# Attention matmuls in 64-row tiles throughout: 64x64 for the scores, 64x32 for values and sums

## The chip, the cores and the metric

The kernel runs as one program on all eight cores of one Trainium2 chip. The cores divide the batch and do not talk to each other. The metric is the device time of the slowest core in microseconds (us). Most executions agree within 0.3%, but a program on eight cores has a second, slower state. In it the cores of one die, sometimes of both, get a lower TensorE clock, and the time is some per cent longer, whatever the kernel. "Mean of the cores" below is the mean of the eight core spans of one profiled fast run. It is steadier than the slowest core, which hops from core to core between runs.

## The reference, cut to what matters

One layer of a streaming encoder: RMS norm, one input projection, two mixers side by side (attention in a sliding window, and a gated MLP that mixes positions in chunks of 128), a gated merge, and a SwiGLU feed-forward. The change touches the attention of the long prompts. There are 16 query heads of 64 and 4 key/value heads; a chunk of 64 queries sees its own chunk and the two before it, and each head has a "sink" in the denominator:

```python
def sink_attention(q, k, v, sinks, mask):
    s = jnp.einsum('...qhgd,...khd->...hgqk', q, k).astype(jnp.float32) * (HEAD_DIM ** -0.5)
    ...
    p = jnp.exp(s - m)
    denom = jnp.sum(p, axis=-1, keepdims=True) + jnp.exp(sk - m)
    p = (p / denom).astype(v.dtype)
    return jnp.einsum('...hgqk,...khd->...qhgd', p, v)
```

A core has two prompts of 4096 rows. It works on them in 16 tiles (t0 to t15) of 512 rows, and each tile in four blocks of 128 rows: 64 blocks. A block has two query chunks (c = 0, 1). Each sees 192 keys: one pair of key chunks lies wholly inside the windows and is done as 128 rows, the third key chunk as 64 rows.

## The kernel before: the parts that matter

The scores are computed transposed (keys on partitions). `PT` holds the exponentials of the 128-key part, `PT3` those of the third key chunk. Values and denominators (a product with a matrix of ones) follow as matmuls. `ps` is PSUM, with eight banks of 128 x 512 FP32.

```python
def S2(b):                                   # scores and exponentials of one block
    for tp in range(2):
        for c in range(2):
            for h in range(2):
                kc0 = c0 + 128 * c
                mm(v4(ps[:, 2 * tp + h, 256 * c:256 * c + 256]),      # tile 64 x 128
                   kT[64 * h:64 * h + 64, tp, kc0:kc0 + 128], qv(tp, h, c), ...)
        act(PT[:, tp, :, cs], ps[:, 2 * tp:2 * tp + 2, cs], AF.Exp, ...)
    ...                                      # third chunk: tiles of 64 x 64, banks 4 and 5
    act(PT3[pr], ps[pr, 4:6, :], AF.Exp, B(4, 5), ["PT3"], scale=0.125)

def PV(n):                                   # 128 x 64 tiles: values, then sums, of the two full chunks
    for use_v in (True, False):
        for c in range(2):
            for h in range(2):
                o = ps[hs, pb + c, 0:256] if use_v else ps[hs, pb + c, 256:512]
                lhs = Vt[:, b + c, vc] if use_v else ones[:, 0:64]
                mm(o, lhs, PT[:, tp, h, 256 * c:256 * c + 256], ...)
    small.append(lambda: PVs(b, tp, first))  # 64 x 64 tiles with PT3: run after both PV calls

def divide(b, tp):                           # twice per block
    act(od, ps[:, pb:pb + 2, :], AF.Copy, ...)
    tt(POOL, d4, d4, esb, ALU.add, ...)
    recip(od[:, :, 256:512], od[:, :, 256:512], ok_, ok_)   # VectorE, 128 x 512
    mults[tp] = ...
```

This is the loop over the four blocks of a tile (G = 0 to 3, which I call blocks 1 to 4), and the order of the gelu units ahead of it:

```python
steps = "v0 v0 u0 v1 v1 u1 u2 v2 v2 u3 b0 u4 s0 b1 u5 s1 | b2 v3 s2 v3 u6 u7".split()   # u, v: gelu
...
for G in range(4):
    S2(G)                                    # scores, exponentials
    ...
    for j, (bl, hf) in enumerate(sp[G]):
        if G:
            seed(hf, 4 + j)                  # ScalarE writes a bias into a PSUM bank
    g_unit(4 * G)                            # 8 dense matmuls of 512 columns, then a tanh on ScalarE
    ...
    g_unit(4 * G + 1)
    PV2(G)                                   # values and sums
    ...
    g_unit(4 * G + 2)
    if N and N["turned"]:
        if G in (1, 2):
            turned_square(N, G)              # ScalarE squares rows of the next tile
    ...
    g_unit(4 * G + 3)
    if N and N["turned"] and G == 0:
        turned_square(N, 0)
```

The softmax here doesn't subtract the row's maximum and nothing guards it: scores larger than these inputs give would overflow.

## Time and profile before

| before | value | view |
|---|---|---|
| time, 3 runs | 4013.2 fast; 4354.0 and 4628.99 slow | times |
| spans of the cores, profiled run (fast) | 4008.7 to 4015.0, mean 4011.2 us | table of cores |
| granted TensorE clock | 0.997 to 0.999 | table of cores |
| TensorE / VectorE / ScalarE / GpSimd busy | 99% / 44% / 35% / 20% | page |
| attention matmuls of the prompts, busy | 229 us, 5.7% | list of groups |

From the page of the profiled run: the busy time of the engines, the chain of work that ended last, and one group (line, engine, operation, out<-in, shapes, count | busy us, mean ns | idle before and its releaser).

```profile
span 4015.0 us, 60008 instructions; the slowest of 8 cores (4008.7 to 4015.0 us)
...
PE 3962.1 (99%) x22234; PEld 1893.3 (47%) x22630; DVE 1752.7 (44%) x1725; ACT 1390.4 (35%) x2144; POOL 806.8 (20%) x1028
...
PE 97%; issue 1%; DMA 1%; DVE 0%; ACT 0%; POOL 0%; DVEq 0%; SPq 0%; POOLq 0%; ACTq 0%
...
L334 DVE RECIPROCAL tmp<-tmp 128x512 f32<-128x512 f32 x129 | 421.9, 3311 | 127.4 <-POOL tmp L319 127.3
...
```

TensorE is busy 99% of the span and makes up 97% of the chain. Only time that TensorE itself saves counts directly; the VectorE reciprocals, although they add up to 422 us, are not on the chain.

One block on TensorE, from the timeline (start us, length us, engine, line, operation, out<-in, tile, shapes, count):

```profile
...
2086.73 0.95 PE L300 MATMUL ps<-qT,kT 64*128 64x256 bf16 x16
2087.61 3.63 PE L300 MATMUL ps<-hT,ring 128*128 128x512 bf16 x16
2091.17 0.41 PE L300 MATMUL ps<-PT,Vt 128*64 128x256 bf16 x4
2091.41 0.38 PE L300 MATMUL ps<-PT,ones 128*64 128x256 bf16 x4
2091.63 0.39 PE L300 MATMUL ps<-PT,Vt 128*64 128x256 bf16 x4
2091.85 0.39 PE L300 MATMUL ps<-PT,ones 128*64 128x256 bf16 x4
2092.16 0.30 PE L300 MATMUL ps<-PT,Vt 64*64 64x256 bf16 x4
...
2092.51 0.28 PE L300 MATMUL ps<-PT,ones 64*64 64x256 bf16 x4
2092.73 0.62 PE L300 MATMUL ps<-WmT,mgT 128*128 128x128 bf16 x8
```

The length of a group contains the flow of its last matmul, so I read starts. From the first score (2086.73) to the next dense matmul (2087.61) is 0.88 us; from the first value (2091.17) to the next work (2092.73) is 1.56 us. A "round" is a set of matmuls that use different parts of the array at the same time; a round of 256 columns takes 0.109 us. Before, a block has 4 + 2 rounds of scores and 8 + 4 rounds of values and sums.

This is block 1 of tile t9, ScalarE and then TensorE:

```profile
...
2323.04 0.60 ACT L309 ACTIVATE big<-ps 128x512 bf16<-128x512 f32 x1 [1.13 <-PE ps L300]
2323.66 1.28 ACT L309 ACT_TABLE_LOAD   x1
2324.95 2.85 ACT L309 ACTIVATE PT<-ps 128x1024 bf16<-128x1024 f32 x3
...
```

### The profile page before, as it was taken

How to read it: one execution, taken by the hardware profiler on the slowest of the kernel's cores; microseconds unless marked ns; L12 is line 12 of the kernel's file. 1: busy time of each engine (PE TensorE's matmuls, PEld its weight loads, DVE VectorE, ACT ScalarE, POOL GpSimd, SP SyncE). 2: the span in 40 equal slices, each digit the busy share in tenths (PEclk: the TensorE clock that was granted, in tenths of full speed). 3: DMA queues.
4: the chain of work that ended last, by engine and by line, in shares of the span. 5: the costliest groups of instructions: out<-in, count | busy, mean ns of one | idle time of the engine just before them, and what ended most of it. 6: DMA issues, size and time to landing. Idle time of an engine off the chain costs nothing.

```text
span 4015.0 us, 60008 instructions; the slowest of 8 cores (4008.7 to 4015.0 us)
## 1 busy us (share of the span) xinstructions
PE 3962.1 (99%) x22234; PEld 1893.3 (47%) x22630; DVE 1752.7 (44%) x1725; ACT 1390.4 (35%) x2144; POOL 806.8 (20%) x1028
## 2 busy tenths in 40 slices
PE   8999999999999999999999999999999999999998
PEld 4544445444444444444444444444444444444444
DVE  4616426163361633616345262442615426163352
ACT  5515325153241423314243142522515224152331
POOL 3204123040220302202031120311203012030220
PEclk9999999999999999999999999999999999999999
DMA  9999998885664645537455464654646445464442
GB/s 174 186 186 210 193 200 217 216 236 160 195 202 154 223 153 181 194 138 232 147 192 184 144 211 163 203 168 161 209 148 208 168 171 198 150 219 151 176 145 81
DMA packets 128326, 727.58 MB, mean 181 GB/s; under 512 B 20142, under 2 KB 22666, under 8 KB 58538
## 3 DMA queue, kind: packets, MB, share of 16 engines
q1 hardware_dynamic: 105088, 603.72, 44.3%
q0 software_dynamic: 15856, 95.57, 14.9%
q10 hardware_dynamic: 7098, 24.42, 1.5%
q8 instruction: 188, 3.08, 0.3%
q14 instruction: 96, 0.79, 0.1%
HBM read 749.06 MB, written 70.08 MB: 204 GB/s over the span
## 4 chain that ended last, share of the span: by engine, by line
PE 97%; issue 1%; DMA 1%; DVE 0%; ACT 0%; POOL 0%; DVEq 0%; SPq 0%; POOLq 0%; ACTq 0%
PE ps L300 96%; PE ps L304 1%; DMA gx<-xp 0%; DMA s_rs<-stt 0%; DVE tmp L330 0%; ACT PT L309 0%; DMA aT<-vecs 0%; DVE hT L330 0%; DMA hst<-s_rs 0%; POOL stt L319 0%; DVE big L330 0%; ACT hst L309 0%; ACT big L309 0%; SPq L136 0%; DVE hst L330 0%
## 5 line engine op out<-in xcount | busy, mean ns | idle before, releaser
L300 PE MATMUL ps<-aT,ring 128*128 128x512 bf16 (+1 forms) x6551 | 1446.0, 378 | 9.6 <-ACT aT L309 1.4
L309 ACT ACTIVATE tmp<-ps 128x512 f32<-128x512 f32 (+2 forms) x614 | 463.1, 765 | 1612.9 <-PE ps L300 1611.7
L300 PEld LDWEIGHTS ps<-aT,ring 128*128 128x128 bf16 x6704 | 655.2, 98 | 774.1 <-issue 1.6
L300 PE MATMUL ps<-hT,ring 128*128 128x512 bf16 x4206 | 965.7, 379 | 12.2 <-issue 3.2
L319 DVE TENSOR_TENSOR big<-ps,tmp 128x512 bf16<-128x512 f32 x352 | 243.2, 691 | 972.4 <-PE ps L300 920.3
L300 PEld LDWEIGHTS ps<-hT,ring 128*128 128x128 bf16 x4352 | 414.1, 98 | 485.8 <-issue 19.9
L300 PE MATMUL ps<-ring,big 128*128 128x512 bf16 x2756 | 605.8, 379 | 3.2
L326 POOL TENSOR_SCALAR stt<-stt 128x1 f32<-128x1 f32 (+2 forms) x289 | 139.0, 481 | 2186.0 <-ACT tmp L309 1777.9
L334 DVE RECIPROCAL tmp<-tmp 128x512 f32<-128x512 f32 x129 | 421.9, 3311 | 127.4 <-POOL tmp L319 127.3
L330 DVE SCALAR_TENSOR_TENSOR tmp<-ps,stt,gS 128x1024 f32<-128x1024 f32 x123 | 157.9, 1283 | 700.0 <-POOL stt L319 679.9
L300 PEld LDWEIGHTS ps<-ring,big 128*128 128x128 bf16 x2816 | 275.2, 98 | 332.6 <-issue 1.3
L300 PE MATMUL ps<-ring,hT 128*128 128x512 bf16 (+1 forms) x1518 | 293.2, 344 | 1.1 <-issue 0.2
L309 ACT ACTIVATE big<-ps 128x512 bf16<-128x512 f32 (+1 forms) x389 | 226.0, 596 | 190.3 <-PE ps L300 186.8
L300 PE MATMUL ps<-big,ring 128*128 128x512 bf16 x1021 | 235.4, 379 | 1.3 <-DVE tmp L330 1.1
L300 PE MATMUL ps<-ring,mgT 128*128 128x512 bf16 x1008 | 225.9, 379 | 2.0 <-DVE mgT L319 1.2
L309 ACT ACTIVATE qT<-ps 128x512 bf16<-128x512 f32 (+1 forms) x132 | 80.1, 606 | 412.0 <-PE ps L300 411.7
L300 PEld LDWEIGHTS ps<-ring,hT 128*128 128x128 bf16 x1536 | 148.1, 98 | 124.2 <-issue 1.3
L319 POOL TENSOR_TENSOR stt<-stt,negh 128x1 f32<-128x1 f32 (+1 forms) x292 | 184.4, 632 | 52.6 <-DVE stt L326 8.7
L319 POOL TENSOR_TENSOR aT<-tmp 128x512 bf16<-128x512 f32 x112 | 142.1, 1269 | 257.6 <-DVE tmp L334 253.3
L309 ACT ACTIVATE PT<-ps 128x1024 bf16<-128x1024 f32 (+1 forms) x192 | 180.7, 1018 | 0.3
L330 DVE SCALAR_TENSOR_TENSOR tmp<-big,ps 128x1024 f32<-128x1024 bf16 x128 | 155.5, 1215 | 54.8 <-PE ps L300 54.8
L319 POOL TENSOR_TENSOR xt<-xt,tmp 128x1024 f32<-128x1024 f32 x60 | 141.6, 2360 | 92.2 <-DVE tmp L330 92.2
(164 smaller groups left out, 2289.6 us busy)
## 6 DMA issues: line engine op xcount, KB each, us to landing
ring<-s_wfi SPq DMA_DIRECT2D x145, 1024.0 KB, 5.5
ring<-s_win SPq DMA_DIRECT2D x136, 1024.0 KB, 6.1
ring<-wb POOLq DMA_DIRECT2D x84, 1024.0 KB, 19.0
ring<-s_wfo SPq DMA_DIRECT2D x58, 1024.0 KB, 4.8
xt<-xp SPq DMA_DIRECT2D x63, 512.0 KB, 11.3
ring<-s_wap SPq DMA_DIRECT2D x30, 1024.0 KB, 7.3
ring<-s_wgp SPq DMA_DIRECT2D x29, 1024.0 KB, 7.4
ring<-s_wout SPq DMA_DIRECT2D x29, 1024.0 KB, 8.8
```

The source lines that it names most:

```text
L300: m.op(PE, lambda e: e.matmul(out, lhsT=lhsT, rhs=rhs, start=start, stop=stop, skip_group_check=True), reads=reads, writes=[("ps", bank)])
L304: m.op(PE, lambda e: e.transpose(out=out, in_=in_, identity=idn), reads=reads + ["ident"], writes=[("ps", TB)])
L309: m.op(ACT, lambda e: e.activation(out=out, in_=in_, func=func, scale=scale, **kw), reads=reads, writes=writes)
L319: m.op(eng, lambda e: e.tensor_tensor(out=out, in0=in0, in1=in1, op=op), reads=reads, writes=writes)
L326: m.op(eng, lambda e: e.tensor_scalar(out=out, in0=in0, scalar1=s1, scalar2=s2, op0=op0, op1=op1), reads=reads, writes=writes)
L330: m.op(DVE, lambda e: e.scalar_tensor_tensor(out=out, in0=in0, scalar=scalar, in1=in1, op0=op0, op1=op1), reads=reads, writes=writes)
L334: m.op(DVE, lambda e: e.reciprocal(out=out, in_=in_), reads=reads, writes=writes)
```

## The change

The intent: use only tiles of 64 rows, so that the array is cut the same way throughout a stage and more tiles run at once. Scores become 64x64 (four tiles at once, still six rounds). Values and sums become 64x32: eight tiles at once, nine rounds instead of twelve. Sums now lie in banks of their own (2 and 3), which saves one reciprocal, one eviction and two GpSimd adds per block and costs two VectorE adds. The two row halves never write one bank at the same time: each writes a bank of its own, and halfway they exchange banks; the exchange is guarded by a wait of TensorE on its own semaphore.

```diff
-                        for h in range(2):
-                            kc0 = c0 + 128 * c
-                            mm(v4(ps[:, 2 * tp + h, 256 * c:256 * c + 256]),
-                               kT[64 * h:64 * h + 64, tp, kc0:kc0 + 128], qv(tp, h, c), True, True, KK + QK,
-                               2 * tp + h)
+                        for j in range(2):
+                            for h in range(2):
+                                kc0 = c0 + 128 * c + 64 * j
+                                mm(v4(ps[64 * j:64 * j + 64, 2 * tp + h, 256 * c:256 * c + 256]),
+                                   kT[64 * h:64 * h + 64, tp, kc0:kc0 + 64], qv(tp, h, c), True, True, KK + QK,
+                                   2 * tp + h)
...
+                def tiles(which, out, lhs, lk):        # one round: 2 row halves x 4 heads
+                    for r in range(2):
+                        rs = slice(64 * r, 64 * r + 64)
+                        c = (0, 1, r)[which]           # which 0, 1: PT; 2: PT3
+                        ...
+                        for k in range(4):
+                            ...
+                            mm(ps[32 * k:32 * k + 32, bank, 256 * c:256 * c + 256], lhs(rs, sl, k, r), p, ...)
...
+                sums(0)
+                values(0, 0)
+                values(0, 1)
+                values(0, 2)                           # fourth round: needs PT3
+                swap_at = len(m.ops[PE]) - 1
+                sums(1)
+                sums(2)
+                if ordered:
+                    m.self_wait(PE, swap_at)
+                values(1, 0)                           # row halves write the other's bank
+                values(1, 1)
+                values(1, 2)
...
+                act(od, ps[:, 0:2, :], AF.Copy, B(0, 1), ok_)
+                tt(DVE, v4(t), v4(ps[:, 2, :]), esb, ALU.add, B(2) + ["es2"], tk)
+                tt(DVE, t[:, cs], ps[:, 3, cs], t[:, cs], ALU.add, B(3) + tk, tk)
+                recip(t, t, tk, tk)
```

Cut: the same for the short sample rows, the new order of the sinks and of the projection's rows that follows from the 32-column tiles, and the small method that records the self-wait.

## The prediction

> All times are for the fast state: before 4013.2 us, 4015.0 us in the profile, granted clock 0.998.
>
> **What bounds the kernel.** TensorE: busy 99% of the span, and 97% of the chain of waits. VectorE is busy 44%, ScalarE 35%, GpSimd 20%. Only time that TensorE itself saves or loses counts.
>
> **Attention on TensorE now.** The attention matmuls (qT·kT, PT·Vt, PT·ones, two shapes each) are busy 229 us, 5.7% of the span (list of groups). The timeline from 2086 to 2093 us shows one block of 128 rows: scores start at 2086.73, the next dense matmul at 2087.61 (0.88 us); values and sums start at 2091.17, the next work at 2092.72 (1.55 us). A block repeats every 10.0 us; there are 64.
> Matmuls on different tiles run together: one round of 256 columns, whether two 128x64, two 64x128 or four 64x64 tiles, takes 0.109 us (start to start). Before: 4+2 rounds of scores, 8+4 of values and sums. The Trainium skill ("TensorEngine Tiling (Array Packing)", Key Properties) says that a change of tiling mode drains the array. The trace agrees: over a change, start to start is about 0.09 us longer than a round, and the next round 0.02 longer. There are six changes per block.
>
> **What the change does on TensorE.** Scores are 64x64 throughout: six rounds, one mode change less. Values and sums become 72 matmuls of 64x32, eight tiles at once: nine rounds instead of twelve, one change less. Four 32-column tiles did run together in the sample rows (0.22 us per four at 512 columns); I expect eight to. Instruction supply should hold: the trace shows a matmul and its weight load dispatched in about 9 ns, so 8 pairs need 75 ns of a round's 109.
> Saved per block: 3 x 0.109 + 2 x 0.115 = 0.56 us.
> Lost: the skill's Restrictions (Gotcha 1) say that different row tiles may not use one bank at once, hence the self-wait. Its matmul lies two rounds before it. A matmul ends 0.27 us after its start and a semaphore needs about 0.1 us to be seen and passed, against 0.33 us of cover: an estimated 0.10 us lost per block. The third exponential ends 0.1 us after values start today and will be needed 0.35 us after; it should just fit.
> Net 0.46 us x 64 = 29 us.
>
> **Elsewhere, off the path.** Per block one reciprocal of 128x512 less (3.31 us VectorE), two adds from PSUM more (0.69 us each): VectorE about -120 us. ScalarE loses one 1.0 us eviction per block, GpSimd two 1.0 us adds (-130 us). Score banks 2 and 3 are now freed by VectorE, about 0.5 us before the next scores want them. Weights are only reordered; the sample path is negligible.
>
> **Predicted:** 3984 us (-0.7%), 3968 to 4006. Faster by over 2%: 0.02; within 2%: 0.96; slower: 0.02.
>
> **What would show it.** Blocks repeat every 9.5 to 9.6 us. Scores to next dense about 0.78 us, values and sums to the next work about 1.2 us. Eight 64x32 matmuls start within 0.03 us; rounds 0.11 us apart, one gap of 0.2 us at the self-wait. Reciprocals x65 instead of x129; VectorE busy about 1630 us, GpSimd about 680.
>
> **What would make it wrong.** Eight tiles not running together, or 144 instructions in 1 us starving the queue: values and sums stay at 1.5 us and nothing is gained. A late third exponential or late VectorE adds, as PE idle with those as releaser. A self-wait costing 0.3 us or more. A lower granted clock from denser array use.

## More of the kernel before

```profile
...
2327.32 0.41 PE L300 MATMUL ps<-PT,Vt 128*64 128x256 bf16 x4
...
2328.32 0.30 PE L300 MATMUL ps<-PT,Vt 64*64 64x256 bf16 x4
...
```

The last gelu of the tile is followed by a load of ScalarE's function table (1.28 us), and only then do the three exponentials run, until 2327.80. Values start at 2327.32, so the third exponential is 0.48 us late for a start of values. It does no harm here, because the old order uses it only in the last four rounds, at 2328.32, 1.00 us after values start.

## The result, and the profile after

The changed kernel ran in 4003.42, 4003.16 and 4003.45 us, and once in the slow state (4696.96; die 1 had a clock of 0.837). In the same rounds the kernel before took 4013.2 and 4012.5 us fast (4354.0 and 4628.99 slow). The ratio of the fast runs is 0.9976, with a 95% interval of 0.9953 to 0.9998. Here and below a ratio is the mean time of one kernel's fast runs over that of the other's fast runs of the same rounds, so it is not quite the ratio of the medians quoted. The forecast was "within 2%", which is right, and 4003.4 lies in the stated range. But the gain is 0.24%, a third of the 0.7% that was forecast: about 10 us on the slowest core and 12.7 us in the mean of the cores of the two profiled runs (4011.2 to 3998.5), instead of 29. Over all undisturbed fast runs the kernel before has means of 4008.8 to 4011.4 and the changed kernel, in its three fast runs here, 3998.5 to 3998.9, so the gain is 10 to 13 us.

The page after, the same parts, with the queue that brings instructions (packets, MB, share):

```profile
span 4001.9 us, 66201 instructions; the slowest of 8 cores (3995.3 to 4001.9 us)
...
PE 3966.1 (99%) x25670; PEld 1879.1 (47%) x25670; DVE 1630.8 (41%) x1790; ACT 1333.1 (33%) x2080; POOL 678.6 (17%) x900
...
q8 instruction: 211, 3.46, 0.3%
...
PE 97%; ACT 1%; issue 1%; DMA 1%; DVE 0%; POOL 0%; DVEq 0%; POOLq 0%; ACTq 0%
...
L342 DVE RECIPROCAL tmp<-tmp 128x512 f32<-128x512 f32 (+1 forms) x65 | 215.5, 3316 | 6.7
...
```

The reciprocals are x65, VectorE is busy 1630.8 us and GpSimd 678.6 us, as predicted. TensorE is still 99% busy. The queue q8 moved 188 packets before and 211 now: each is 16,384 bytes, and the 23 more are what 2 x 3,000 further TensorE instructions of 64 bytes need. And there is a wait that was hardly there before, in the list of groups by form:

```profile
...
L308 PE MATMUL ps<-PT,Vt 64*32 64x256 bf16 x3024 | 69.1, 271 | 4.8 <-ACT PT L317 3.0 <-issue 1.8
...
```

TensorE idles 3.0 us before value matmuls because of `PT`, the exponentials (14 times), and 1.8 us because of "issue", which is time in which it waited for nothing that the profile shows.

Where the blocks changed, start to start, is the same on all cores. These are medians over the tiles (not t0 and t8, whose first block is shorter):

| per block, us | before | after | predicted |
|---|---|---|---|
| scores to next dense matmul | 0.886 | 0.782 | 0.78 |
| values and sums to next work, block 1 | 1.558 | 1.674 | 1.2 |
| the same, block 2 | 1.558 | 1.284 | 1.2 |
| the same, blocks 3 and 4 | 1.558 | 1.268 | 1.2 |
| from there to the next scores, block 1 | 3.560 | 3.557 | unchanged |
| the same, block 2, tiles t4 to t14 | 4.006 | 4.333 | unchanged |
| the same, block 3 | 4.006 | 4.004 | unchanged |

Scores came out to the nanosecond. Values miss by 0.07 us in the good blocks, and two parts went the wrong way altogether: the values of block 1, and the tail of block 2. Here is block 1 of t9 after, first ScalarE, then TensorE:

```profile
...
2318.74 0.60 ACT L317 ACTIVATE big<-ps 128x512 bf16<-128x512 f32 x1 [1.13 <-PE ps L308]
2319.35 1.28 ACT L317 ACT_TABLE_LOAD   x1
2320.64 2.86 ACT L317 ACTIVATE PT<-ps 128x1024 bf16<-128x1024 f32 x3
...
```

```profile
...
2322.91 0.30 PE L308 MATMUL ps<-PT,ones 64*32 64x256 bf16 x8
2323.03 0.40 PE L308 MATMUL ps<-PT,Vt 64*32 64x256 bf16 x16
2323.64 0.30 PE L308 MATMUL ps<-PT,Vt 64*32 64x256 bf16 x8 [0.21 <-ACT PT L317]
2323.75 0.41 PE L308 MATMUL ps<-PT,ones 64*32 64x256 bf16 x16
2324.13 0.52 PE L308 MATMUL ps<-PT,Vt 64*32 64x256 bf16 x24
2324.58 0.61 PE L308 MATMUL ps<-hT,ring 128*128 128x512 bf16 x2
```

The third exponential ends at 2323.50 (2320.64 + 2.86), 0.59 us after values start. The fourth round needs it 0.34 us after. TensorE stops in front of that round and goes on at 2323.64 with "<-ACT PT". In the other blocks it is in time: in block 2 of t4 to t14 the third exponential ends 0.20 us after the start of values (0.10 before the change), everywhere else in blocks 2 to 4 it ends at least 0.8 us ahead of it. The table load stands only in front of block 1. In the first block of each prompt (t0 and t8), which is shorter, there is no wait either: 14 tiles are left.

Block 2 of t9, TensorE and then ScalarE:

```profile
...
2328.14 0.85 PE L308 MATMUL ps<-qT,kT 64*64 64x256 bf16 x24
2328.92 3.63 PE L308 MATMUL ps<-hT,ring 128*128 128x512 bf16 x16
2332.48 0.30 PE L308 MATMUL ps<-PT,ones 64*32 64x256 bf16 x8
2332.60 0.53 PE L308 MATMUL ps<-PT,Vt 64*32 64x256 bf16 x24
2332.93 0.41 PE L308 MATMUL ps<-PT,ones 64*32 64x256 bf16 x16
2333.31 0.52 PE L308 MATMUL ps<-PT,Vt 64*32 64x256 bf16 x24
2333.76 0.66 PE L308 MATMUL ps<-WmT,mgT 128*128 128x128 bf16 x8
2334.55 3.61 PE L308 MATMUL ps<-hT,ring 128*128 128x512 bf16 x16
...
```

```profile
...
2328.80 1.05 ACT L317 ACTIVATE hst<-gx 128x1024 bf16<-128x1024 f32 x1
...
2329.84 2.84 ACT L317 ACTIVATE PT<-ps 128x1024 bf16<-128x1024 f32 x3
2332.77 1.12 ACT L317 ACTIVATE ps<-bsb 128x512 f32<-128x512 bf16 x2
2333.83 1.06 ACT L317 ACTIVATE big<-ps 128x512 bf16<-128x512 f32 x2
...
```

The rounds start 0.11 us apart (2332.48, 2332.60, ...), except for one longer step in front of the last group: 2332.93 to 2333.31 holds two rounds of sums and the self-wait. In single instructions, an undisturbed block has its rounds at 0, 0.120, 0.229, 0.338, 0.447, 0.556, then 0.815 after the self-wait, 0.923, 1.031, and the next work at 1.269. The self-wait step is 0.259 instead of 0.109, so it costs 0.150 us. Then the tail: the eight 128x128 matmuls start at 2333.76 and the next dense unit only at 2334.55, 0.79 us later; undisturbed this is 0.46 (before the change in the median of the complete traces, and in experiment 5 below). ScalarE is the reason. Between 2328.80 and 2334.9 it works without a pause: a square of the next tile (1.05), three exponentials (2.84), two bias seeds (1.12), and only then the tanh that empties the PSUM bank which the dense unit wants. Before, the same chain ended just in time, because values took 0.27 us longer.

The last loss has no releaser. In tiles t0 to t3 TensorE stops now and then for up to 2.0 us, mostly within values and sums (2.6 us per core) and in the attention of the sample rows in t0 (1.7 us). This one is on core 3 in tile t1, from the timeline:

```profile
...
376.41 0.40 PE L308 MATMUL ps<-PT,Vt 64*32 64x256 bf16 x12
377.75 0.40 PE L308 MATMUL ps<-PT,Vt 64*32 64x256 bf16 x12 [0.94 <-issue]
...
```

Twelve of the last 24 value matmuls start in time and the other twelve 1.2 us too late, with "issue" as what ended it. If I number TensorE's instructions (a matmul and its weight load are two, each wait is one more), every such stop lies at number 179 or 180 modulo 256, and 256 instructions of 64 bytes are one 16,384-byte packet of q8. Near this stop a packet of q8 starts at 375.41 and takes 0.90 us; TensorE went on 1.44 us after its end. The Trainium skill ("Runtime: NRT & Kernel Launch", Instruction fetch mechanics) says that instructions are fetched in blocks of 16 KiB, 256 instructions, and that crossing a boundary is mostly hidden. The trace agrees with the size of the block. It does not agree with "hidden" here: stops at that number add up to 4.5 us per core (0.1 us before). Those in the sample rows, about 1.1 to 2.6 us together on a core, lie in a path that the prediction called negligible.

### The profile page after: what moved, and what is told of

It reads as the page before. It is cut to its first block, busy times and chain, and to the rows that moved or that the text cites. A ratio compares the mean times of both kernels' runs of the same rounds, so it can differ in the third digit from the quotient of the medians.

```text
span 4001.9 us, 66201 instructions; the slowest of 8 cores (3995.3 to 4001.9 us)
## 1 busy us (share of the span) xinstructions
PE 3966.1 (99%) x25670; PEld 1879.1 (47%) x25670; DVE 1630.8 (41%) x1790; ACT 1333.1 (33%) x2080; POOL 678.6 (17%) x900
## 4 chain that ended last, share of the span: by engine, by line
PE 97%; ACT 1%; issue 1%; DMA 1%; DVE 0%; POOL 0%; DVEq 0%; POOLq 0%; ACTq 0%
PE ps L308 96%; ACT PT L317 1%; PE ps L312 1%; DMA ring<-wb 0%; DMA aT<-vecs 0%; DVE tmp L338 0%; DVE hst L338 0%; ACT L317 0%; POOL stt L327 0%; DVE PT L338 0%; DVEq L161 0%; DVE tmp L327 0%; DVE xt L338 0%; ACT gS L317 0%; ACT aT L317 0%
## 5 line engine op out<-in xcount | busy, mean ns | idle before, releaser
L308 PE MATMUL ps<-aT,ring 128*128 128x512 bf16 x6704 | 1455.0, 377 | 1.4 <-ACT aT L317 1.4
L308 PE MATMUL ps<-hT,ring 128*128 128x512 bf16 x4352 | 991.0, 380 | 4.2 <-DMA ring<-wb 2.8
L317 ACT ACTIVATE tmp<-ps 128x512 f32<-128x512 f32 (+1 forms) x550 | 404.1, 735 | 1614.7 <-PE ps L308 1612.3
L342 DVE RECIPROCAL tmp<-tmp 128x512 f32<-128x512 f32 (+1 forms) x65 | 215.5, 3316 | 6.7
L327 DVE TENSOR_TENSOR big<-ps,big 128x512 bf16<-128x512 f32 x128 | 86.8, 689 | 200.5 <-PE ps L308 196.9
```

The source lines that it names most:

```text
L308: m.op(PE, lambda e: e.matmul(out, lhsT=lhsT, rhs=rhs, start=start, stop=stop, skip_group_check=True), reads=reads, writes=[("ps", bank)])
L317: m.op(ACT, lambda e: e.activation(out=out, in_=in_, func=func, scale=scale, **kw), reads=reads, writes=writes)
L327: m.op(eng, lambda e: e.tensor_tensor(out=out, in0=in0, in1=in1, op=op), reads=reads, writes=writes)
L342: m.op(DVE, lambda e: e.reciprocal(out=out, in_=in_), reads=reads, writes=writes)
```

## The experiments

The theory that I formed from the two traces: the 16 us that are missing are a sum of separate losses. The self-wait is dearer than planned; block 1 waits for ScalarE; block 2's tail waits for ScalarE; and instruction fetch stops TensorE more. The theory of the ScalarE waits and the theory of instruction fetch are often named by the letters S and F. The main rivals: the tiles themselves are dearer than a round suggests (drain or array conflicts), so that the loss sits in every block; and whatever is won moves to the next wait.

I call "fetch stops" the sum of TensorE's unexplained losses at instruction numbers 178 to 181 modulo 256: what a step from start to start takes beyond the ordinary step at such a place, where that is over 0.1 us, as a mean of the cores whose trace is complete. The expectations used a cruder count, every gap above 0.1 us at these numbers. Ordinary steps from round to round are 0.105 to 0.13 us, so it gave 1.2 us for the kernel before, where only one stop of 0.43 us on one core is real, and about 5 us for the changed kernel.

### 1. Scores alone

The kernel before with only the new score loop (the first hunk of the diff).

> The kernel before with only the scores changed to 64x64. Theory S (ScalarE gives the gain back: TensorE now reaches points where it needs ScalarE results sooner than ScalarE has them) expects the full 0.104 us of each of 64 blocks, because the old order needs the third exponential only after eight rounds: 6.2 to 6.7 us, about 4006.5 us, scores to next dense work 0.78 us, values 1.56 us everywhere. Rival T (the small tiles themselves yield less than planned, nothing else) expects the same here; what tells them apart is whether this gain and that of the values alone add up to the whole.

Measured: 4006.54 to 4008.32 us fast, ratio 0.9985 (0.9962 to 1.0007). Scores 0.782 us, values 1.558 as before, block 2's tail 4.059, no fetch stop. The score half of the change gives its 0.104 us per block (6.7 us in 64 blocks) and nothing is lost but 0.05 us in block 2's tail: already here ScalarE has no slack left.

### 2. Values and sums alone

The changed kernel with the old 64x128 score loop.

> The changed kernel with the scores back in 64x128. Theory S: in the first block of a tile the wait for the third exponential shrinks by 0.10 (values 1.57 us), in the second block the work after the values drops from 4.33 to 4.23 us, so giving up the scores costs only about 4 us: 4007 us. Rival T: the parts add, so 6.6 us are lost: 4010 us, and values in the first block stay at 1.67 us.

Measured: 4008.9 to 4009.55 us fast, ratio 0.999 (0.9967 to 1.0012). Block 1's values take 1.566 us instead of 1.674 and block 2's tail 4.24 instead of 4.333. Nothing in these values changed: they are 0.1 us faster because the slower scores start them 0.1 us later. This is what a wait on ScalarE does and a price of the tiles does not. The total is 2 us longer than the ScalarE theory said and nearer to the rival's 4010; fetch stops are 6.3 us, 1.8 more than in the changed kernel. By the sum of the single gains, the totals do not speak for the theory: about 6.5 us (experiment 1) and 4 us (this one) add up to the 10 us of the whole. The block times decide between the two, and there the rival's 1.67 us did not come.

### 3. No exchange of banks, no self-wait (wrong result)

The last three rounds write the banks of the sums, with other weights. The result is wrong (relative error 0.10), the number and shapes of the matmuls are the same.

```diff
-                if ordered:
-                    m.self_wait(PE, swap_at)
-                values(1, 0)
-                values(1, 1)
-                values(1, 2)
+                def own(which):
+                    tiles(which, lambda r: 2 + r, lambda rs, sl, k, r: ones[rs, 32:64], lambda sl: "ones")
+                own(0)
+                own(1)
+                own(2)
```

> Wrong result on purpose: the last three rounds write each row half's own bank (2 or 3), with ones as weights, so no bank changes hands and no self-wait is needed. Same matmul count and shapes. Expected gap between rounds 6 and 7: 0.109 in place of 0.259 us, values 1.12 us in a block that waits for nothing else. Theory S: nothing gained in the second block of tiles 4 to 14, where ScalarE is the limit (the work after the values grows to 4.48 us): 7 to 8 us in all, about 3996 us. Rival T (the self-wait is the main loss and all of it is on the path): 64 x 0.15 = 9.6 us, 3993.8 us.

Measured: 3998.09 to 4004.18 us fast, ratio 0.997 (0.9948 to 0.9993), mean of the cores 3994.4. Values in blocks 3 and 4 take 1.109 us: nine rounds of eight tiles at their full pace. So the tiles cost what a round costs, and the exchange costs 0.16 us per block. Of the 10 us that this should save (0.16 x 64), 4.1 show in the mean of the cores: the tail of block 2 grew to as much as 4.49 us (the ScalarE theory said 4.48), and fetch stops rose from 4.5 to 8.4 us. Part of this gain is handed on to the next wait.

### 4. Bias seeds on VectorE instead of ScalarE

This takes 1.12 us out of ScalarE's chain in front of block 2's tail. (It also needed a wait of ScalarE for its own earlier square, to stay free of races.)

```diff
-                        seed(hf, 4 + j)
+                        seed(hf, 4 + j, DVE)
```

> The changed kernel with the bias copies into PSUM (two of 0.56 us per block, on ScalarE between the third exponential and the gate tanh) moved to VectorE, which idles then. Theory S: in the second block of tiles 4 to 14 the work after the values goes from 4.33 to 4.00 us, nothing changes in the first block (values stay 1.67 us): 3.6 us gained, about 3999.7 us. Rival (VectorE's adds free the banks late): it gets worse in the second block, above 4.33 us.

Measured: 4001.37 and 4003.78 us fast, ratio 0.9973 (0.9944 to 1.0002); block 2's tail 4.221 us, not the 4.00 expected. The timeline of VectorE, and then of TensorE, in block 2 of t9 shows why:

```profile
...
2331.53 1.29 DVE L324 CAST ps<-bsb 128x512 f32<-128x512 bf16 x2 [3.57 <-ACT PT L317]
...
```

```profile
...
2332.51 0.84 PE L308 MATMUL ps<-WmT,mgT 128*128 128x128 bf16 x8
2333.19 3.62 PE L308 MATMUL ps<-hT,ring 128*128 128x512 bf16 x16
...
```

The wait for the tanh is gone, but VectorE's two seeds start only after the third exponential (2331.53, "<-ACT PT") and take 0.68 us each, so the 128x128 matmuls (2332.51), which add to the seeds, wait instead: 0.84 us long instead of 0.62. The repair moved the wait from one engine to another. That ScalarE's chain is the cause is not refuted by this, but not shown either; the next run does it without a new wait.

### 5. The square of the next tile earlier

The square that stood at the end of block 1, right before block 2's exponentials, goes one dense unit earlier, where ScalarE has time. Its input is loaded earlier, too.

```diff
-                if N and N["turned"] and G == 0:
-                    N["c"] = stat(8)
-                    turned_square(N, 0)
...
-                    if G in (1, 2):
-                        turned_square(N, G)
+                    if G == 0:
+                        N["c"] = stat(8)
+                    if G < 3:
+                        turned_square(N, G)
```

> The changed kernel with one ScalarE square of 1.05 us (a norm of the next tile, which stands just before the exponentials of the second block) put earlier, into ScalarE's idle time of the first block, and its load earlier. The moved-bias run took away the late tanh but met a new wait for the bias copies (4.22 in place of 4.00 us); this one moves the work that delays both. Theory S: work after the values of the second block 4.33 to 4.00 us in tiles 4 to 14, its values 1.284 to 1.268, the first block unchanged (1.67): 3.6 to 3.8 us gained. Rival (not ScalarE's order but VectorE or the banks): stays at 4.33.

Measured: 3999.16, 3999.66 and 4002.49 us fast, ratio 0.996 (0.994 to 0.9979), on a chip where the kernel before took 4012.8 to 4020.45. Block 2's tail is 4.004 us, block 1 is unchanged. ScalarE and TensorE in block 2 of t9:

```profile
...
2327.83 1.05 ACT L317 ACTIVATE hst<-gx 128x1024 bf16<-128x1024 f32 x1
...
2329.56 2.85 ACT L317 ACTIVATE PT<-ps 128x1024 bf16<-128x1024 f32 x3
2332.50 1.12 ACT L317 ACTIVATE ps<-bsb 128x512 f32<-128x512 bf16 x2
2333.56 1.06 ACT L317 ACTIVATE big<-ps 128x512 bf16<-128x512 f32 x2
...
```

```profile
...
2334.50 0.62 PE L308 MATMUL ps<-WmT,mgT 128*128 128x128 bf16 x8
2334.96 3.62 PE L308 MATMUL ps<-hT,ring 128*128 128x512 bf16 x16
...
```

The square (2327.83) now runs before the tanh that precedes the exponentials; exponentials and seeds start 0.27 us earlier, and the dense unit follows 0.46 us after the 128x128 matmuls. One moved line of ScalarE removes the whole loss of 0.33 us: it was ScalarE's chain.

### 6. Block 1 later against ScalarE

One spatial unit (bias seed and four 128x128 matmuls) goes from before the last gelu units to after them, in front of the scores; two VectorE operations are put off behind it.

```diff
-                steps = "... | b2 v3 s2 v3 u6 u7".split()
+                steps = "... | v3 v3 B2 u6 u7 S2".split()      # B, S: seed and spatial unit in bank 7
```

> The changed kernel with one spatial step (four 128-column matmuls, 0.24 us, no ScalarE work after it) moved behind the last gelu unit of a tile, so that ScalarE's table load and the first block's exponentials start 0.24 us earlier against TensorE. Two layer-norm operations on VectorE move behind it, so that its bank comes free. Theory S: values of the first block 1.67 to about 1.45 us in tiles 1 to 15, nothing else changes: 3 to 3.6 us gained. Rival (the first block is long for the small tiles or the self-wait): stays 1.67.

Measured: 4000.19 and 4001.6 us fast, ratio 0.9961 (0.9937 to 0.9985), mean of the cores 3994.8. Block 1's values take 1.450 us instead of 1.674, everything else is as in the changed kernel.

```profile
...
2320.33 0.30 PE L308 MATMUL ps<-PT,ones 64*32 64x256 bf16 x8
2320.45 0.70 PE L308 MATMUL ps<-PT,Vt 64*32 64x256 bf16 x24
2320.95 0.41 PE L308 MATMUL ps<-PT,ones 64*32 64x256 bf16 x16
...
```

The number of matmuls and the tiles of block 1 are unchanged, only the time at which it comes, measured against the table load, and its values lose 0.22 us. The wait is ScalarE's, and 0.18 us of it are left (1.450 against 1.268).

### 7. One more round under the self-wait

In blocks 3 and 4 the first round of sums goes behind the three value rounds, so that three rounds instead of two lie between the matmul that the self-wait waits for and the wait.

```diff
+                early = b >= 2
+                if not early:
+                    sums(0)
-                sums(0)
                 values(0, 0)
                 values(0, 1)
                 values(0, 2)
                 swap_at = len(m.ops[PE]) - 1
+                if early:
+                    sums(0)
                 sums(1)
```

> The changed kernel with the first round of sums put after the three first rounds of values in blocks 3 and 4 of each tile (where the third exponential is ready in time): three rounds in place of two lie between the exchange and the self-wait. The gap at the wait measured 0.259 us with two rounds; with one round more, 0.109 us of it is covered: gap 0.15, values 1.16 us in these 32 blocks, 1.268 in the second: 3.5 us gained.

Measured: one fast run, 4006.98 us; the others were slow, so there is no ratio. Values in blocks 3 and 4 take 1.160 us, 0.108 less: exactly one round of cover more, one round of wait less. The total does not show it. Fetch stops are 7.8 us instead of 4.5, and the tiles before t4 took about 4 us longer, these stops included. Block by block it is a clear result, for the whole kernel an inconclusive one. Even between t4's and t15's first scores, where 22 such blocks should save 2.4 us, the mean of the complete cores falls by only 0.4 us: in the dense work after the attention TensorE waits for VectorE (`tmp`, then `hT`) in some tiles of single cores, up to 0.9 us at once in the complete traces, which makes this work 1.7 us longer per core than in the changed kernel.

### 8. Shift the instruction boundaries

98 matmuls of one column at the start (196 instructions), nothing else.

> The changed kernel with 98 one-column matmuls (196 instructions) at the start, where TensorE waits for its first weights. In the traces every unexplained gap inside the values lies at TensorE instruction 179 or 180 modulo 256, the size of one 16 KB instruction packet, in tiles 1 to 4, where the DMA engines are busiest. Theory F (instruction fetch): moved by 196, no such place falls into the values of tiles 1 to 4, so no gap over 0.3 us there, 1 to 3 us gained on a core. Rival (a semaphore or a bank): the gaps stay at the same matmuls.

Measured: 4012.51 and 4017.53 us fast, ratio 0.9996 (0.9972 to 1.002). The stops left the values of blocks 3 and 4 from t1 on, which now take 1.268 us in the median and in the mean, and turned up in scores, in dense matmuls and in the values of t0, again at numbers 179 to 181 modulo 256, for up to 2.7 us. Fetch stops are 9.2 us, and the mean of the cores is 4005.7, 7 us above the changed kernel's. So the stop belongs to the number of the instruction and not to the kind of matmul: the first half of the expectation held. The second half, that shifting them would gain time, was wrong.

### 9. The repairs together, with the reordered sums

Experiments 5 and 6, and the order of experiment 7 in blocks 2 to 4.

> The three mends together: the square earlier (e5), one spatial step between the last gelu and the first scores (e6), and three rounds of cover for the self-wait in blocks 2 to 4 (e7). Theory S expects them to add, since each removes another wait: first block's values 1.45, the others' 1.16, work after the second block's values 4.00 us. That is 3.7 + 3.3 + 48 x 0.109 = 12 us less per core than the changed kernel, if instruction fetch costs the same 5 us a core; the slowest core about 3991 us, with 3 us of scatter from the fetch.

Measured: six of eight runs were slow, and no ratio can be formed. The two fast runs took 3998.13 and 4003.46 us. Blocks as expected: block 1 1.45 us, the others 1.160, block 2's tail 4.004. In the profiled run die 0 was undisturbed, with spans of 3986.2 to 3997.7 us, and fetch stops of 7.2 to 10.0 us on its cores whose trace is complete. The expected 3991 us for the slowest core was missed by 7 and 12 us. In the mean of the cores the two fast runs are at 3991.7 and 3992.9, about 6 us below the changed kernel's 3998.5 instead of 12; about 3 to 5 us of the rest can be the additional fetch stops that die 0 shows.

### 10. The changed kernel once more

> The changed kernel once more, on the chip of this call, to compare the combined version and the split one with it: 4003.5 us, spans of the cores 3995 to 4002 us, up to 5 us more if this chip's DMA is slower.

Measured: one fast run, 4009.13 us, the rest slow. Die 1 was undisturbed in the profiled run: 3995.2 to 4001.5 us, blocks as in the first run. Fetch stops are 3.6 us. The time of the changed kernel thus varies by 6 us between fast runs, more than most of the effects looked for here. The block times do not vary, which is why the argument is built on them.

### 11. Only more instructions

The kernel before, with each matmul of 256 columns in values and sums split into two of 128 columns: 64 matmuls per block instead of 32, nearly the 72 of the changed kernel, but with the old tiles.

> The kernel before with each 256-column matmul of values and sums split into two of 128 columns: same tiles, same columns streamed, same order and waits, but 64 matmuls and weight loads in place of 32 per block. Theory F (what the small tiles lose to instruction fetch comes from the number of TensorE instructions) expects the gaps at instruction 179 or 180 modulo 256 to grow from 1.2 us per core to 3 to 6 us, values 1.56 to about 1.6 us otherwise. Rival (the gaps belong to 64x32 tiles or to the bank exchange): they stay near 1 us.

Measured: 4016.61 to 4018.15 us fast, ratio 0.9997 (0.9948 to 1.0046); values 1.601 us as expected; but fetch stops of 0.8 us (0.1 before), where 3 to 6 were expected, though the critical number fell into the values of t1 and t3. So the number of instructions alone does not do it. (The ratio counts one run of the kernel before, 4042.81 us, as fast, although one die had a clock down to 0.990 in it; without that run it is 1.0012.) The two kernels differ in pace: about 144 instructions in 1.27 us after the change, 128 in 1.60 us here. That pace in front of the boundary decides is an inference and was not tested on its own.

### 12. The two ScalarE repairs together

Experiments 5 and 6 without the reordered sums.

> The changed kernel with both repairs of the ScalarE waits that were tried singly (square of the next tile moved early; first spatial unit of the first block moved in front of the exponentials), and without the reordered sums. The theory (the shortfall is a sum of separate ScalarE waits, so the repairs add): first block's values 1.45 us, the other blocks' 1.268, tail of block 2 4.00; mean span of the cores about 3991.5 us with about 5 us of instruction-fetch gaps (3998.5 of the changed kernel, less 0.33 x 11 and 0.22 x 15), the slowest core about 3996 to 4000, ratio to before about 0.9955. The rival (slack won in one place only moves the wait to the next one): the blocks shrink as said but the mean of the cores stays near 3995, as in the single repairs.

Measured: 3997.43 to 4001.59 us in four fast runs, ratio 0.9958 (0.9941 to 0.9974). Blocks: block 1 1.450 us, the others 1.268, block 2's tail 4.004, all as the theory said. The mean of the cores is 3994.9 in the profiled run, which is the rival's number and not the theory's 3991.5. But that run was the slowest of the four: the other three have 3993.1, 3992.3 and 3992.3, and the mean of all four is 3993.1, between the two. Taken the same way, over all fast runs, the changed kernel has 3998.8 (three runs), experiment 5 3995.3 and experiment 6 3995.6: single gains of 3.5 and 3.2 us, together 5.7, though on different chips. In the profiled runs the stretch from t4's first scores to t15's first scores tells more; there the DMA traffic of the start is over (mean of six cores):

| us | before | after | 5: square | 6: block 1 | 12: both |
|---|---|---|---|---|---|
| t4 to t15 | 2705.7 | 2695.3 | 2691.7 | 2693.4 | 2690.6 |
| fetch stops, whole span | 0.1 | 4.5 | 5.1 | 4.6 | 6.3 |

Alone, the repairs won 3.6 and 1.9 us there, together 4.7: they add, nearly, and no new wait opened in the blocks. By the blocks alone 6 us would be saved there. What is missing lies in the dense work between them: after the attention of t5 to t11 TensorE waits for VectorE on some cores (`tmp`, then `hT`), up to 3.2 us at once, and this work is 1.6 us longer per core than in the changed kernel. So the rival is right in part: slack won at ScalarE can end at VectorE. What also kept the profiled total up lies before t4, which took 1.3 us longer with 1.8 us more of fetch stops. By the intervals this version is faster than the kernel before; against the changed kernel (0.9976) it is lower in the ratio, but the intervals overlap.

## Why the prediction was right or wrong

**Right.** TensorE bounds the kernel, and the time stayed within 2%. The scores: 0.782 us for a predicted 0.78. Eight 64x32 tiles run together: the eight matmuls of a round start within 0.023 us, 3.3 ns apart, and rounds are 0.109 us apart. The work off the path: x65 reciprocals, VectorE 1630.8 us for "about 1630", GpSimd 678.6 for "about 680". The clock did not fall.

**Wrong, and by how much.** The prediction's sum was 0.46 us x 64 = 29.4 us. Worked out for the mean of the cores:

| term | as the prediction put it | what the runs showed | us per core |
|---|---|---|---|
| self-wait and exit | "an estimated 0.10 us lost per block", values "about 1.2" | self-wait 0.150, values 1.268 | 0.068 x 64 = 4.3 |
| third exponential | "it should just fit" | true in blocks 2 to 4, not in block 1 (0.406 us more) | 0.406 x 14 = 5.7 |
| ScalarE elsewhere | only "loses one 1.0 us eviction per block" | block 2's tail +0.33 us in t4 to t14 | 0.33 x 11 = 3.6 |
| instruction supply | "should hold" | fetch stops 4.5 instead of 0.1 us | 4.4 |
| left of 29.4 | | measured: 12.7 in the profiled pair, 10 to 13 over the fast runs | 11.4 |

*The third exponential* ("it should just fit") is the step that failed most: it is the largest of the losses. I had read its end in one block, a block 2 (0.1 us after the start of values), and taken it for all 64. In block 1 a table load of 1.28 us stands in front of it, and it ends 0.48 us after values start before the change, 0.59 after it. The old order had 1.00 us of matmuls in front of its first use; the new order has 0.34, because it is used in the fourth of nine rounds. Experiments 2 and 6 showed it. The Trainium skill ("ScalarE: Activation LUTs", What ACT_TABLE_LOAD costs) would have warned me: it gives 1283 ns for the load and a further 1380 ns of drain for every switch of the function set. The trace has 1.28 us for the load; a drain does not show in it, since the gelu ends at 2319.34, the load starts at 2319.35 and the exponentials at 2320.64.

*ScalarE was counted as off the path.* It was busy 35%, but in the 6 us around block 2 it never paused. Shortening values by 0.27 us brought the dense unit forward, and the tanh that had to free its bank did not come forward with it. Experiment 5 showed it. The skill ("TensorEngine Tiling (Array Packing)", PSUM Bottleneck) says that tiling speeds up TensorE but not the emptying of PSUM; this agrees, with 0.33 us per block 2.

*The self-wait* has the right mechanism and the wrong size: 0.150 instead of 0.10 us. The figures in the prediction (0.27 and 0.1 us against 0.33) give only 0.04. The mis-sized term is the 0.1 us for the semaphore: the last matmul of the fourth round starts at 0.361 (0.338 and 0.023) and ends 0.27 later, and the round behind the wait starts at 0.815, another 0.18 us later. Experiment 3 (0.16 us gone with it) and experiment 7 (one more round of cover takes 0.108 us off) show both mechanism and size. The skill (same page, Gotcha 1) asks for the synchronisation of row tiles that meet in one bank; no run here tried the exchange without it.

*Instruction supply* was estimated from the rate at which TensorE dispatches (75 ns for eight pairs; the pairs of a round start 3.3 ns apart in the trace, so this was cautious), and that rate did hold: rounds keep their 0.109 us. What I had not thought of is the arrival of the instructions. Experiment 8 shows that the stops follow the instruction's number; experiment 11 shows that more instructions alone do not cause them. What exactly triggers one remains open.

## What to carry to other kernels

When a change brings an engine's work closer together, read the slack of every producer at every place where the loop body differs, not in one typical block: here one table load in the first block and one square in the second took back 9 of the 29 us. An engine at 35% may still have a stretch without any pause, and there it is the limit as soon as the other engine gets faster. Small effects are best settled by start-to-start times inside the trace, whose medians repeated here to 0.003 us, while whole fast runs of one kernel differed by 6 us.

## What the Trainium skill lacked or had wrong

- "Runtime: NRT & Kernel Launch" (Instruction fetch mechanics) calls the crossing of a 16 KiB instruction block mostly hidden. Here it was not: stops of up to 2.0 us on TensorE at one fixed number modulo 256, 4.5 us per core in the changed kernel, nearly all of them in the first tiles, and up to 9.2 us in an experiment; in experiments 2 and 3 more than half of them (3.5 of 6.3 us, 4.9 of 8.4 us) came in t4 or later. The page gives as its reason that instructions are dispatched more slowly than they are fetched, at about 20 cycles each. It does not say at what pace the crossing shows; the runs only exclude the mere number of instructions (0.8 us with split matmuls).
- "ScalarE: Activation LUTs" (What ACT_TABLE_LOAD costs) adds 1380 ns of drain to the load's 1283 ns. The trace shows 1.28 us for the load and about 0.01 us on either side of it.
- "TensorEngine Tiling (Array Packing)" (Key Properties) says that a change of tiling mode drains the array but gives no figure: here about 0.09 us more, start to start, over a change.
- The same page (Gotcha 1) asks for synchronisation between row tiles that share a bank but has no price for it: a self-wait two rounds after the matmul that it waits for costs 0.150 us, and one further round of 0.109 us between them took 0.108 us off.
- The same page (Instruction Overhead) gives about 60 cycles per matmul and does not say how this counts for tiles that run together. It is no price per matmul there: eight 64x32 matmuls of 256 columns start 3.3 ns apart, which is near the 4 ns per tile of "TensorE: Matmul & The Clock Gate" (Part 3).
